# A decoder layer in one kernel: half steps in three segments, load buffers by stage, bank copies ordered ahead of splits

## The chip, the cores and the metric

The kernel runs on one core of a Trainium2 chip. The metric is the device time of one execution in microseconds (us). PE, DVE, ACT, POOL and SP are the names that the profile gives to TensorE, VectorE, ScalarE, GpSimd and SyncE; SP issues nearly all loads here.

## What is computed

Four steps act on x, 256 tokens of width 2048, in float32. The first and the last are SwiGLU half steps, and these two are what the change touches; an attention and gated-linear-attention mixer and a cross-attention lie between them.

```python
def swiglu(h, w_gate, w_up, w_down):
    return (jax.nn.silu(h @ w_gate) * (h @ w_up)) @ w_down

x = x + 0.5 * swiglu(rms_norm(x, ffn1_norm[l]), ffn1_w_gate[l], ffn1_w_up[l], ffn1_w_down[l])
x = x + hybrid_mixer(rms_norm(x, mix_norm[l]), pos, w_in[l], ...)
x = x + cross_attention(rms_norm(x, xattn_norm[l]), rms_norm(mem, mem_norm[l]), ...)
x = x + 0.5 * swiglu(rms_norm(x, ffn2_norm[l]), ffn2_w_gate[l], ffn2_w_up[l], ffn2_w_down[l])
```

The gate and up matrices are 2048 x 5632, the down matrix is 5632 x 2048.

## The kernel before

**Precision.** Each float32 operand is split in two parts of a narrower kind: `hi` is a cast (ACT) and `lo` the remainder (DVE). A product is three matmuls, hi by hi, hi by lo and lo by hi. So every 1 MB weight tile of 128 x 4 x 512 (a "raw" tile) is loaded, then split in two halves, each with one ACT cast into `wh` and one DVE subtraction into `wl` (`wgroup`, L127 and L128; `parts`, L174 and L175). There are four `wh` and four `wl` half buffers, so the splits run at most four halves ahead of PE.

**A half step** (`ffn`). The 5632 columns are eleven blocks f of 512. Block 0 is done plainly: a gate projection and an up projection (`proj`), eight raw tiles. The other ten go through `seven`: the upper half of the depth of gate and up is treated as a 2 x 2 block product in seven multiplications instead of eight. Write b11, b21 for the first two raw tiles of gate and b12, b22 for those of up. DVE adds b21, then b12, then b22 into b11 (`add`, L180), and POOL adds a tile from memory into b12 by a DMA (`add_hbm`, L184). In PE's order, the products P1 to P6 take b11+b21, b21, b11+b21+b12, b22, all four, and b12; four plain tiles follow, with a last product P7 on b12 before the fourth of them. A product is 12 matmuls of 128 x 128 by 512 columns and a plain tile 24, so a block has 180. Five of the products take differences of x blocks, which `differences` makes once per half step: POOL adds hi and lo of four x blocks (L212) and subtracts them in pairs (L217), ACT and DVE split the results `Fh`, `Fl` (L220, L221).

Four PSUM banks Y, Z, X, R collect the products. Between products Y is copied out by ACT (s21, L234; s22, L240; s12, L249), and DVE joins the banks (L245, L252, L253, L257). Then ACT takes silu of the gate (L366), DVE multiplies by the up part (L372), and `turn` transposes the result on PE (L343) and splits it as `hTh`, `hTl` (L261, L262), the left operand of the down projection.

**Segments.** `SEGS` does blocks 0 to 5, then their down projection in four column chunks, then blocks 6 to 10 and their down projection. At the end of a chunk DVE adds the two banks into x (L379). The turned blocks of a segment must stay in on-chip memory until its last chunk.

**What sets the order.** Each engine runs its own list in order, written by a scheduler from program order and priorities: weight loads and splits stand at `WPRI` = 200 ahead of program order, the first loads at 100000. `later(n, fn)` puts work n half-tiles back in PE's order; `turn` uses 1. A pool hands out buffers: `up` has 34 tiles of 2 KB per partition for everything of medium life, `wp` has `RB` = 5 raw tiles, from which b11, b12 and b22 come as well as the tiles that only pass through. A load waits on SP's list until its buffer is free, and the loads behind it wait too. At the start, ten warm-up matmuls (L413) run on a constant tile while the first loads are under way; x itself is loaded in four chunks at L434 for the norm factor r, which the first silu needs.

Of the kernel before, what the change touches and what calls it, by code (L numbers as in the profile page):

```python
# [27 lines left out]
WPRI = 200  # L28
WARM = 10
# [12 lines left out]
UB = 34  # L42
SB = 8
RB = 5
SEGS = (range(0, 6), range(6, NF))
# [3 lines left out]
def layer_kernel(ctx: ExitStack, tc: tile.TileContext, A: dict, out: bass.AP):  # L49
# [5 lines left out]
    up = ctx.enter_context(tc.tile_pool(name="up", bufs=UB))  # L55
# [4 lines left out]

    def U(shape, dt, name):
        return up.tile(shape, dt, tag="u", name=name)
# [30 lines left out]
    with tc.high_priority(100000):  # L93
        SY.dma_start(gain, A["gains"])
        for g in range(3):
            raw = wp.tile([P, 4, 512], F32, tag="raw", name="raw", bufs=RB)
# [64 lines left out]
    def load(W, c, g):  # L161
        with tc.high_priority(WPRI):
            raw = wp.tile([P, 4, 512], F32, tag="raw", name="raw", bufs=RB)
            SY.dma_start(raw, W[c, g])
        return raw
# [19 lines left out]

    def mms(bank, form, half, start, stop):
# [18 lines left out]
    def differences():  # L205

        x = {}
        for c in range(2):
            for t in range(TT):
                x[t, c] = U([P, 4, P], F32, "xf")  # L210
                hi, lo = (p[:, :, t * P:(t + 1) * P].bitcast(F32) for p in xT[c])
                G.tensor_tensor(x[t, c], hi, lo, op=ALU.add)  # L212
        r = {}
        for name, a, b in (("22-21", (1, 1), (1, 0)), ("12-21", (0, 1), (1, 0)), ("22-12", (1, 1), (0, 1)),
                           ("21-11", (1, 0), (0, 0)), ("11-12", (0, 0), (0, 1))):
            d = W2([P, 4, P], "d")
            G.tensor_tensor(d, x[a], x[b], op=ALU.subtract)  # L217
            hi = U([P, 4, P], F32R, "Fh")
            lo = U([P, 4, P], F32R, "Fl")
            SC.copy(hi, d)  # L220
            V.tensor_sub(lo, d, hi.bitcast(F32))  # L221
            r[name] = (hi, lo)
        return r

    def seven(W1, W2_, f, F, A12, A21, rest):


        Y, Z, X, R = [pa.tile([P, 512], F32, tag="acc", name="acc") for _ in range(4)]
        b11 = load(W1, f, 0)
        b21 = load(W1, f, 1)  # L230
# [3 lines left out]
        SC.copy(s21, Y)  # L234
        b12 = load(W2_, f, 0)
# [4 lines left out]
        SC.copy(s22, Y)  # L240
        b22 = load(W2_, f, 1)
# [3 lines left out]
        V.tensor_sub(s22, R, s22)  # L245
        product(Y, F["21-11"], b12, False)
        add_hbm(b12, W1[f, 0])
        s12 = W2([P, 512], "s12")
        SC.copy(s12, Y)  # L249
        for g in (2, 3):  # L250
            plain((R, X), (rest(0, g), rest(1, g)), load(W2_, f, g), (False, False), (1, 0))
        V.tensor_sub(s12, R, s12)  # L252
        V.tensor_add(s22, X, s22)  # L253
        plain((Y, Z), (rest(0, 2), rest(1, 2)), load(W1, f, 2), (False, False), (1, 0))
        product(Y, F["11-12"], b12, False)
        plain((Y, Z), (rest(0, 3), rest(1, 3)), load(W1, f, 3), (False, False), (0, 1))
        V.tensor_add(s21, Z, s21)  # L257
# [75 lines left out]
    def ffn(pre, r, after, fine=None, last=False):  # L333
        wg, wu, wd = (A[f"{pre}_w_{n}"] for n in ("gate", "up", "down"))
        hT = {}

# [12 lines left out]

        def lhs_h(k, t):  # L350
            return tuple(p[:, k % 4] for p in hT[k // 4, t])

        for seg in SEGS:
            for f in seg:
                if f == 0:
# [3 lines left out]
                    F = differences()  # L359
                else:  # L360
                    y, s21, s12, s22 = seven(wg, wu, f, F, x_block(0, 1), x_block(1, 0), x_block)
                    acc = [y, s21]
                sg = []
                for t in range(TT):
                    s = acc[t] if f and t else W2([P, 512], "sg")
                    SC.activation(s, acc[t], AF.Silu, scale=r[:, t:t + 1])  # L366
                    sg.append(s)
                acc = [s12, s22] if f else proj(wu, f, lhs_x, range(4))
                hs = []
                for t in range(TT):  # L370
                    h = acc[t] if f else W2([P, 512], "h")
                    V.scalar_tensor_tensor(h, acc[t], r[:, t:t + 1], sg[t], op0=ALU.mult, op1=ALU.mult)  # L372
                    hs.append(h)
                later(1, lambda f=f, hs=hs: turn(f, hs))
# [31 lines left out]
    mhalf = con.tile([P, P], F32, name="mhalf")  # L406
    V.memset(mhalf, -0.5)

# [598 lines left out]
```

## Time and profile before

| what | us |
|---|---|
| median of 3 runs (1962.8 to 1963.9) | 1963.34 |
| the profiled execution's own time | 1964.76 |
| its span, first to last instruction | 1962.7 |
| PE busy | 1933.6 |
| DVE busy | 1366.8 |
| ACT busy | 1064.6 |
| POOL busy | 110.6 |

The span is cut by the work as follows: the first block of the first half step and the way into `seven` fill 0 to 82 us; `seven` runs from 82 to 260, 422 to 600, 1302 to 1480 and 1641 to 1820; the down projections lie at 260 to 422, 600 to about 740, 1480 to 1641 and 1820 to the end; the mixer and the cross-attention lie between about 740 and 1240.

How to read it: matmuls overlap, so a matmul's own duration of 390 ns says little, and the distance from one start to the next says much. A busy share near 100% on PE hides matmuls that start late by a fraction of their length. In rows of the timeline, a bracket at the end gives the idle time of that engine before the instruction, and who ended it.

### The profile page before, as it was taken

The page shows a single profiled execution, that of the slowest core. Times are in us where ns is not written, and L with a number is a line of the kernel's source. Part 1 is how long each engine was busy: PE and PEld are TensorE (multiplying, and loading weights), DVE is VectorE, ACT ScalarE, POOL GpSimd, SP SyncE. Part 2 cuts the span into 40 slices and gives each one's busy share as a digit, 9 for nine tenths or more (in the row PEclk, how much of TensorE's full clock was granted, in tenths as well). Part 3 has the DMA queues.
Part 4 walks back from the last instruction along what each step waited for, and adds up shares of the span by engine and source line. Part 5 has one row for each costly group of instructions (what it writes and reads, how often), then busy time and mean ns, then how long its engine had stood idle before and what let it go on. Part 6 is the DMA issues. An engine that isn't in the chain of part 4 may idle for free.

```text
span 1962.7 us, 22466 instructions
## 1 busy us (share of the span) xinstructions
PE 1933.6 (99%) x8760; PEld 1582.1 (81%) x8760; DVE 1366.8 (70%) x1388; ACT 1064.6 (54%) x1305; POOL 110.6 (6%) x99
## 2 busy tenths in 40 slices
PE   8899999999999999999999999999999999999999
PEld 6688788888778888878888889778778888877887
DVE  6788874578887554646775665878886457888643
ACT  5556653355665445544576545656665335666532
POOL 4100000000000000001221000300000000000000
PEclk9899999999999999999999999999999999999999
DMA  8466565556667554535466553556657555666652
GB/s 343 153 211 236 195 238 194 194 207 216 220 209 241 204 182 154 178 129 209 172 215 214 188 184 143 178 190 232 210 199 256 193 193 194 229 202 212 237 214 84
DMA packets 60566, 395.24 MB, mean 201 GB/s; under 512 B 6795, under 2 KB 7947, under 8 KB 14252
## 3 DMA queue, kind: packets, MB, share of 16 engines
q1 hardware_dynamic: 56428, 370.74, 51.6%
q0 software_dynamic: 2880, 20.97, 5.8%
q10 hardware_dynamic: 1152, 2.10, 0.3%
q8 instruction: 68, 1.11, 0.2%
q14 instruction: 38, 0.31, 0.0%
HBM read 391.69 MB, written 2.10 MB: 201 GB/s over the span
## 4 chain that ended last, share of the span: by engine, by line
PE 68%; DVE 20%; DMA 6%; issue 5%; ACT 1%; SPq 0%; DVEq 0%; ACTq 0%
PE acc L138 17%; PE acc L136 17%; PE acc L137 17%; DVE wl L175 13%; DMA raw<-in_ffn_w_gate_dram 6%; PE acc L191 5%; PE acc L190 5%; PE acc L189 5%; DVE raw L180 3%; DVE s L372 1%; ACT wh L174 1%; DVE hTl L262 1%; DVE wl L128 1%; PE tp L343 0%; PE tp L302 0%
## 5 line engine op out<-in xcount | busy, mean ns | idle before, releaser
L128 DVE TENSOR_TENSOR wl<-raw,wh 128x1024 fp32r<-128x1024 f32 (+1 forms) x370 | 459.4, 1246 | 367.8 <-ACT wh L127 365.4
L127 ACT CAST wh<-raw 128x1024 fp32r<-128x1024 f32 (+1 forms) x370 | 386.5, 1048 | 441.0 <-PE acc L138 400.6
L174 ACT CAST wh<-raw 128x1024 fp32r<-128x1024 f32 x440 | 457.8, 1053 | 308.8 <-PE acc L191 274.6
L175 DVE TENSOR_TENSOR wl<-raw,wh 128x1024 fp32r<-128x1024 f32 x440 | 522.2, 1223 | 94.1 <-ACT wh L174 91.0
L189 PE MATMUL acc<-wh,xTh 128*128 128x512 f32 x800 | 314.4, 393 | 3.5 <-ACT sg L366 2.3
L190 PE MATMUL acc<-wl,xTh 128*128 128x512 f32 x800 | 314.2, 393 | 1.5 <-DVE wl L175 0.8
L191 PE MATMUL acc<-wh,xTl 128*128 128x512 f32 x800 | 313.6, 392 | 0.0
L136 PE MATMUL acc<-wh,hTh 128*128 128x512 f32 x704 | 274.6, 390 | 0.0
L138 PE MATMUL acc<-wh,hTl 128*128 128x512 f32 x704 | 274.0, 389 | 0.0
L137 PE MATMUL acc<-wl,hTh 128*128 128x512 f32 x704 | 274.0, 389 | 0.0
L136 PE MATMUL acc<-wh,xTh 128*128 128x512 f32 x544 | 215.0, 396 | 5.4 <-ACT wh L127 2.8
L137 PE MATMUL acc<-wl,xTh 128*128 128x512 f32 x544 | 212.5, 391 | 2.6 <-DVE wl L128 2.6
L138 PE MATMUL acc<-wh,xTl 128*128 128x512 f32 x544 | 212.0, 390 | 0.7 <-DVE xTl L286 0.7
L189 PEld LDWEIGHTS acc<-wh,xTh 128*128 128x128 f32 x800 | 150.4, 188 | 42.3 <-ACT wh L174 9.3
L190 PEld LDWEIGHTS acc<-wl,xTh 128*128 128x128 f32 x800 | 150.4, 188 | 40.0 <-DVE wl L175 9.3
L191 PEld LDWEIGHTS acc<-wh,xTl 128*128 128x128 f32 x800 | 150.5, 188 | 30.3
L180 DVE TENSOR_TENSOR raw<-raw 128x2048 f32<-128x2048 f32 x60 | 137.3, 2289 | 51.2 <-DMA raw<-in_ffn_w_gate_dram 50.5
L191 PE MATMUL acc<-wh,Fl 128*128 128x512 f32 x400 | 157.0, 393 | 4.1 <-DVE Fl L221 4.1
L190 PE MATMUL acc<-wl,Fh 128*128 128x512 f32 x400 | 158.8, 397 | 0.2 <-DVE wl L175 0.2
L189 PE MATMUL acc<-wh,Fh 128*128 128x512 f32 x400 | 157.6, 394 | 0.0
L137 PEld LDWEIGHTS acc<-wl,hTh 128*128 128x128 f32 x704 | 132.2, 188 | 27.4
L138 PEld LDWEIGHTS acc<-wh,hTl 128*128 128x128 f32 x704 | 132.1, 188 | 27.3
(281 smaller groups left out, 1946.5 us busy)
## 6 DMA issues: line engine op xcount, KB each, us to landing
raw<-in_ffn_w_up_dram SPq DMA_DIRECT2D x88, 1024.0 KB, 4.8
raw<-in_ffn_w_down_dram SPq DMA_DIRECT2D x88, 1024.0 KB, 4.8
raw<-in_ffn_w_gate_dram SPq DMA_DIRECT2D x85, 1024.0 KB, 4.9
raw<-in_w_in_dram SPq DMA_DIRECT2D x48, 1024.0 KB, 4.8
raw<-in_ffn_w_gate_dram POOLq DMA_DIRECT2D x20, 1024.0 KB, 9.3
raw<-in_w_out_dram SPq DMA_DIRECT2D x16, 1024.0 KB, 4.8
raw<-in_xattn_w_k_dram SPq DMA_DIRECT2D x4, 1024.0 KB, 5.7
raw<-in_xattn_w_q_dram SPq DMA_DIRECT2D x4, 1024.0 KB, 4.8
```

Source lines behind the costliest of these rows:

```text
L127: SC.copy(wh[:, d], src)
L128: V.tensor_sub(wl[:, d], src, wh[:, d].bitcast(F32))
L136: PE.matmul(acc[t], lh, wh, start=first and i == 0, stop=False)
L137: PE.matmul(acc[t], lh, wl, start=False, stop=False)
L138: PE.matmul(acc[t], ll, wh, start=False, stop=last and i == len(half) - 1)
L174: SC.copy(wh, src)
L175: V.tensor_sub(wl, src, wh.bitcast(F32))
L180: V.tensor_add(dst, dst, src)
L189: PE.matmul(bank, hi[:, k], wh, start=start and i == 0, stop=False, skip_group_check=True)
L190: PE.matmul(bank, hi[:, k], wl, start=False, stop=False, skip_group_check=True)
L191: PE.matmul(bank, lo[:, k], wh, start=False, stop=stop and i == len(half) - 1, skip_group_check=True)
L262: V.tensor_sub(lo, ps, hi.bitcast(F32))
```

## The change

- `SEGS` becomes three segments: blocks 0 to 3, 4 to 7 and 8 to 10, each with its down projection in four chunks.
- The pool for medium tiles is opened anew for each stage (`enter`): 26 tiles in the half steps with three more raw tiles beside them, 32 in the middle. `RB` goes from 5 to 4. b11, b12 and b22 come from the three (`raw_tile(long=True)`), everything else from the four.
- Loads of `seven` go from priority 200 to `LPRI` = 400.
- The bank copies and joins, the silu and the multiplication get priority `FPRI` = 300 (`urgent`), above the splits.
- The differences of x are made by DVE, additions and subtractions alike, three of them one half-tile after block 0's gate projection and two four half-tiles later; the last two are split into the x blocks (1,1) and (0,0) in place.
- `turn` is put back by 2 half-tiles instead of 1; the x chunks' load priorities fall by 12 per chunk instead of 34.
- The warm-up matmuls read a tile `idle` of their own, set by DVE.

```diff
-UB = 34
+UF = 26
+UM = 32
 SB = 8
-RB = 5
-SEGS = (range(0, 6), range(6, NF))
+RB = 4
+RX = 3
+DIFF = 1
+TURN = 2
+SEGS = (range(0, 4), range(4, 8), range(8, NF))
...
+    def raw_tile(long=False):
+
+        if long and "r" in stage:
+            return stage["r"].tile([P, 4, 512], F32, tag="rawx", name="raw")
+        return wp.tile([P, 4, 512], F32, tag="raw", name="raw", bufs=RB)
+
+    enter(u=UF, r=RX)
...
+    def urgent(op, *args, **kw):
+
+        with tc.high_priority(FPRI):
+            op(*args, **kw)
...
+    def difference(x, name, home=None):
+
+        a, b = PAIRS[name]
+        with tc.high_priority(WPRI):
             d = W2([P, 4, P], "d")
-            G.tensor_tensor(d, x[a], x[b], op=ALU.subtract)
-            hi = U([P, 4, P], F32R, "Fh")
-            lo = U([P, 4, P], F32R, "Fl")
+            V.tensor_sub(d, x[a], x[b])
+            hi, lo = home or (U([P, 4, P], F32R, "Fh"), U([P, 4, P], F32R, "Fl"))
             SC.copy(hi, d)
             V.tensor_sub(lo, d, hi.bitcast(F32))
...
-        b11 = load(W1, f, 0)
-        b21 = load(W1, f, 1)
+        b11 = load(ld(0, k1), True)
+        b21 = load(ld(0, k2))
         add(b11, b21)
         product(Y, A21, b11, True)
         s21 = W2([P, 512], "s21")
-        SC.copy(s21, Y)
-        b12 = load(W2_, f, 0)
+        urgent(SC.copy, s21, Y)
+        b12 = load(ld(1, k1), True)
...
-                    F = differences()
+                    later(DIFF, lambda: x_differences(("22-21", "12-21", "22-12")))
+                    later(DIFF + 4, lambda: x_differences(("21-11", "11-12")))
...
-                later(1, lambda f=f, hs=hs: turn(f, hs))
+                later(TURN, lambda f=f, hs=hs: turn(f, hs))
...
-        PE.matmul(wps, mhalf, mhalf, start=True, stop=True)
+        PE.matmul(wps, idle, idle, start=True, stop=True)
...
-            with tc.high_priority(XPRI - 34 * c):
+            with tc.high_priority(XPRI - 12 * c):
                 SY.dma_start(xs[c], A["x"][0, :, c * 512:(c + 1) * 512].rearrange("(t p) d -> p t d", p=P))
```

The scheduler's lists move at three places. The first is SP's list at the start, behind the loads of block 0's first three gate tiles, where both kernels are alike. Before (L117 loads a tile of block 0, L164 one of block 1, `xr` is the transposed x and `x_105` to `x_108` are the four x chunks):

```order
L117 DMA raw<-in_ffn_w_gate_dram 128x2048
L276 DMA xr<-in_xT_dram 128x512 x2
L434 DMA x_105<-in_x_dram 128x2x512
L117 DMA raw<-in_ffn_w_up_dram 128x2048 x2
L434 DMA x_106<-in_x_dram 128x2x512
L117 DMA raw<-in_ffn_w_up_dram 128x2048
L434 DMA x_107<-in_x_dram 128x2x512
L164 DMA raw<-in_ffn_w_gate_dram 128x2048 x2
L434 DMA x_108<-in_x_dram 128x2x512
L164 DMA raw<-in_ffn_w_up_dram 128x2048 x4
```

After (L189 loads for block 1, L142 for block 0, L304 is the transposed x, L480 the x chunks):

```order
L189 DMA raw<-in_ffn_w_gate_dram 128x2048
L189 DMA raw<-in_ffn_w_up_dram 128x2048 x2
L142 DMA raw<-in_ffn_w_gate_dram 128x2048
L304 DMA xr<-in_xT_dram 128x512 x2
L142 DMA raw<-in_ffn_w_up_dram 128x2048
L480 DMA x_108<-in_x_dram 128x2x512
L480 DMA x_109<-in_x_dram 128x2x512
L480 DMA x_110<-in_x_dram 128x2x512
L480 DMA x_111<-in_x_dram 128x2x512
```

Three tiles of block 1 (b11, b12, b22) now stand ahead of block 0's fourth gate tile and of the last quarter of the transposed x, and the x chunks stand closer behind them.

The second place is DVE's list at the passage from block 0 to block 1. Before, from the last split of block 0 to P3's first split (raw_523 is b11, raw_525 b21, raw_568 b12; `Fl_346` and `Fl_352` belong to P2 and P3):

```order
L128 TENSOR_TENSOR wl_500<-raw_481,wh_499 128x1024
L180 TENSOR_TENSOR raw_523<-raw_523,raw_525 128x2048
L322 TENSOR_REDUCE r1t_329<-ss1_308 128x2
...
L175 TENSOR_TENSOR wl_529<-raw_523,wh_528 128x1024
...
L175 TENSOR_TENSOR wl_581<-raw_525,wh_580 128x1024
L180 TENSOR_TENSOR raw_523<-raw_523,raw_568 128x2048
L221 TENSOR_TENSOR Fl_346<-d_343,Fh_345 128x512
L372 SCALAR_TENSOR_TENSOR h_515<-acc_377,r1_333,sg_373 128x512
L221 TENSOR_TENSOR Fl_352<-d_349,Fh_351 128x512
L175 TENSOR_TENSOR wl_592<-raw_523,wh_591 128x1024
```

After, over the same stretch (raw_524 is b11, raw_526 b21, raw_569 b12):

```order
L350 TENSOR_REDUCE r1t_334<-ss1_313 128x2
...
L243 TENSOR_TENSOR d_372<-xf_370,xf_366 128x512
...
L246 TENSOR_TENSOR Fl_375<-d_372,Fh_374 128x512
...
L246 TENSOR_TENSOR xTl0_140<-d_462,xTh0_139 128x4x128
L153 TENSOR_TENSOR wl_501<-raw_482,wh_500 128x1024
L205 TENSOR_TENSOR raw_524<-raw_524,raw_526 128x2048
L214 SCALAR_TENSOR_TENSOR h_516<-acc_344,r1_338,sg_340 128x512
L214 SCALAR_TENSOR_TENSOR h_518<-acc_345,r1_338,sg_342 128x512
L200 TENSOR_TENSOR wl_530<-raw_524,wh_529 128x1024
...
L205 TENSOR_TENSOR raw_524<-raw_524,raw_569 128x2048
L290 TENSOR_TENSOR hTl_550<-tp_551,hTh_549 128x512
...
L200 TENSOR_TENSOR wl_593<-raw_524,wh_592 128x1024
```

All five differences and their remainders now stand ahead of the first addition for block 1, and both multiplications of block 0 stand ahead of P1's first split.

The third place is DVE's list where one block of `seven` ends and the next begins, the third block to the fourth. Before (raw_1173 is b11 of the fourth block, s12_1003 and s22_936 are the third's results):

```order
L180 TENSOR_TENSOR raw_1173<-raw_1173,raw_1218 128x2048
L175 TENSOR_TENSOR wl_1221<-raw_1175,wh_1220 128x1024
L257 TENSOR_TENSOR s21_891<-acc_845,s21_891 128x512
L372 SCALAR_TENSOR_TENSOR s12_1003<-s12_1003,r1_333,sg_1164 128x512
L175 TENSOR_TENSOR wl_1231<-raw_1175,wh_1230 128x1024
L175 TENSOR_TENSOR wl_1242<-raw_1173,wh_1241 128x1024
L372 SCALAR_TENSOR_TENSOR s22_936<-s22_936,r1_333,s21_891 128x512
L175 TENSOR_TENSOR wl_1252<-raw_1173,wh_1251 128x1024
L262 TENSOR_TENSOR hTl_1189<-tp_1190,hTh_1188 128x512
```

After, the same stretch:

```order
L205 TENSOR_TENSOR raw_1174<-raw_1174,raw_1219 128x2048
L200 TENSOR_TENSOR wl_1222<-raw_1176,wh_1221 128x1024
L214 SCALAR_TENSOR_TENSOR s12_1004<-s12_1004,r1_338,sg_1165 128x512
L214 TENSOR_TENSOR s21_892<-acc_846,s21_892 128x512
L200 TENSOR_TENSOR wl_1232<-raw_1176,wh_1231 128x1024
L200 TENSOR_TENSOR wl_1243<-raw_1174,wh_1242 128x1024
L214 SCALAR_TENSOR_TENSOR s22_937<-s22_937,r1_338,s21_892 128x512
L200 TENSOR_TENSOR wl_1253<-raw_1174,wh_1252 128x1024
L290 TENSOR_TENSOR hTl_1200<-tp_1201,hTh_1199 128x512
```

Only the first multiplication and the join of s21 have changed places. In PE's list the transposes of s12 move from behind the eighth matmul of P1 to behind its twelfth, and those of s22 keep their place in P2; the ten warm-up matmuls move from the head of the list to behind the 31st matmul.

96 lines of the change are left out of this document (59 added, 37 removed).

## The prediction

> **What bounds the kernel now.** I read the page first, then the list of waits on PE, the table by stage, and the timelines of the two stages that lose time.
>
> ```profile
> PE 1933.6 (99%) x8760; PEld 1582.1 (81%) x8760; DVE 1366.8 (70%) x1388; ACT 1064.6 (54%) x1305; POOL 110.6 (6%) x99
> ```
>
> PE is busy for 1933.6 of 1962.7 us, so it is the bound, and what a change of order can win is the 29 us of idle PE and matmuls that start late inside its busy time. The table by stage shows where these are.
>
> ```profile
> 0.00:58.00 58.00, 49.91 (x211) 38.76 (x212) 41.36 (x35) 32.85 (x53) 27.83 (x25) 1.00 0.81 309
> 58.00:82.00 24.00, 17.33 (x59) 12.83 (x58) 18.87 (x19) 13.30 (x18) 0.00 (x0) 0.79 0.24 88
> 82.00:260.00 178.00, 176.94 (x784) 142.65 (x783) 153.98 (x138) 111.67 (x124) 4.49 (x5) 1.00 0.65 220
> 260.00:422.00 162.00, 162.00 (x720) 134.06 (x719) 90.42 (x81) 68.58 (x69) 0.00 (x0) 1.00 0.56 200
> 600.00:1230.00 630.00, 630.00 (x3020) 525.26 (x3020) 378.28 (x502) 340.47 (x505) 50.52 (x45) 1.00 0.53 187
> ```
>
> The columns are PE, PE's loads, DVE, ACT and POOL busy, then PE's granted clock, the DMA share and GB/s. From 600 to 1230 and in a down projection (260 to 422) PE has no gap: nothing is to be won there, and DVE is busy for only 90 of 162 us. In `seven` (82 to 260) DVE is busy for 154 of 178 us, and from 58 to 82 PE idles 6.7 us at a mean clock of 0.79. PE's waits name the causes.
>
> ```profile
> PE tp L343 <- DVE s L372: 5.4, 8, 0.9
> PE acc L191 <- DVE Fl L221: 4.1, 1, 4.1
> PE acc L189 <- ACT sg L366: 2.3, 1, 2.3
> PE acc L189 <- ACT wh L174: 0.6, 2, 0.3
> ```
>
> **The passage from block 0 to block 1.** In PE's timeline a matmul's start to the next start is what counts.
>
> ```profile
> 14.28 0.73 PE L136 MATMUL acc<-wh,xTh 128*128 128x512 f32 x2 [1.31 <-ACT wh L127]
> 60.78 0.50 PE L189 MATMUL acc<-wh,xTh 128*128 128x512 f32 x1 [2.30 <-ACT sg L366]
> 62.65 0.63 PE L190 MATMUL acc<-wl,xTh 128*128 128x512 f32 x1
> 63.08 0.63 PE L191 MATMUL acc<-wh,xTl 128*128 128x512 f32 x1
> 73.86 0.79 PE L191 MATMUL acc<-wh,Fl 128*128 128x512 f32 x1 [4.14 <-DVE Fl L221]
> 76.29 0.63 PE L191 MATMUL acc<-wh,Fl 128*128 128x512 f32 x1
> 331.04 0.39 PE L138 MATMUL acc<-wh,hTl 128*128 128x512 f32 x1
> 331.27 0.39 PE L136 MATMUL acc<-wh,hTh 128*128 128x512 f32 x1
> ```
>
> At 331 matmuls start 0.23 us apart, at 62.65 and 63.08 0.43 apart. About eight slow ones follow the 2.30 us gap and about ten the 4.14 us gap: 1.6 and 2.0 us on top of the gaps. The 1.31 us gap at 14.28 had no such price: the granted clock from 10 to 20 us is 1.00 (row further below).
>
> The 4.14 us gap is P3 waiting for a remainder of a difference, which came late from POOL and then stood behind an addition on DVE:
>
> ```profile
> 53.21 3.53 POOL L217 TENSOR_TENSOR d<-xf 128x512 f32<-128x512 f32 x2
> 70.92 2.29 DVE L180 TENSOR_TENSOR raw<-raw 128x2048 f32<-128x2048 f32 x1
> 73.12 0.68 DVE L221 TENSOR_TENSOR Fl<-d,Fh 128x512 fp32r<-128x512 f32 x1
> 88.69 0.57 ACT L249 COPY s<-acc 128x512 f32<-128x512 f32 x1
> ```
>
> P6 ends when the copy of s12 begins, at 88.7; block 0 ended at about 58.4 (60.78 less the gap). So the first six products took 30.3 us, where 72 matmuls and eight transposes need 72 x 0.227 + 0.8 = 17.1.
>
> After the change all differences are done on DVE before P1. Count from U, the end of block 0 on PE. DVE's list has two multiplications, which wait for U, then P1's first split: 1.5 + 1.2, so P1 runs freely from U+2.7, a gap like today's 2.30, with 1.6 us of slow clock (kept). Ahead of P3 DVE has, behind that split, three more splits, the addition of b12, two hTl and P3's own: 4 x 1.22 + 2.29 + 2 x 0.68 = 8.5, so U+11.2. PE needs 24 x 0.227 + 0.8 + 1.6 = 7.9 and comes at U+10.6: 0.6 us of waiting instead of 4.14. P5 needs three more splits, the addition of b22 and its own: 4 x 1.22 + 2.29 = 7.2, U+18.4, where PE comes at U+16.6. P5 and P6 take 5.4, so P6 ends at U+23.8: 6.5 us less than today. The wait of 1.8 us before P5 lies between the 1.31 us that left the clock alone and the 2.30 us that slowed it: 0 to 1.6 us more, of which I take half. That leaves **5.7 us**. [...]
>
> What moves U is the front of SP's list: 3 MB of block 1 go ahead of block 0's fourth gate tile and the last x quarter.
>
> ```profile
> 10.00:20.00 10.00, 7.67 (x32) 5.31 (x31) 7.84 (x9) 6.20 (x9) 6.52 (x5) 1.00 1.02 407
> 20.00:30.00 10.00, 7.48 (x31) 5.18 (x29) 10.00 (x6) 3.69 (x5) 10.00 (x6) 1.00 1.04 427
> 27.30 4.00 POOL L284 TENSOR_TENSOR xr<-xr,gain 128x512 f32<-128x512 f32 x2
> 30.02 0.50 PE L136 MATMUL acc<-wh,xTh 128*128 128x512 f32 x1 [0.98 <-ACT xTh L285]
> ```
>
> At 0.42 MB/us the 3.1 MB cost 7.5 us. Today the fourth group starts at 30.0 because POOL, busy with x additions, scales the last x quarter only from 27.3; those additions leave POOL. By bytes in order, 9.5 MB must land before that quarter is there; some 6 MB have landed at 20, so it is there at 28, POOL and ACT add 1.3 and 0.6: again 30. U stays, within -1 and +5 (the bound if it lands 5 us later).
>
> The additions and subtractions, 4 + 5, cost DVE 0.68 each (L221's price) and lie beside block 0, where POOL's took 1.8 us each (the row at 53.21). Today DVE itself slows beside them:
>
> ```profile
> L128 DVE TENSOR_TENSOR wl<-raw,wh 128x1024 fp32r<-128x1024 f32 x14 | 22.4, 1629 | 6.9 <-ACT wh L127 6.9
> L175 DVE TENSOR_TENSOR wl<-raw,wh 128x1024 fp32r<-128x1024 f32 x85 | 100.3, 1218 | 9.4 <-ACT wh L174 8.8
> ```
>
> A split means 1629 ns up to 62 us and 1218 ns from 100 to 260.
>
> ```profile
> 1.06 4.02 PE L413 MATMUL wps<-mhalf 128*128 128x128 f32 x20 [1.06 <-DVE mhalf L407]
> ```
>
> The warm-up takes 4.0 us before any data is there; behind the 31st matmul it takes between 2 (at twice the clock) and 4, and the fourth group's data, not before 28, covers it: PE's work up to there is 72 matmuls, 16 us, begun at 6.3. If that cover goes, +2 to +4. In the second half step the differences lie beside block 0 as well: 0, within -1 and +2.
>
> **One block to the next in `seven`.** The transposes of s12 mark the blocks: first and last of four in the first run, then of four in the last run.
>
> ```profile
> 113.86 0.66 PE L343 MATMUL tp<-ident,s 128*128 128x128 f32 x4
> 242.61 0.63 PE L343 MATMUL tp<-ident,s 128*128 128x128 f32 x4 [0.65 <-DVE s L372]
> 1677.46 0.63 PE L343 MATMUL tp<-ident,s 128*128 128x128 f32 x4
> 1807.78 0.63 PE L343 MATMUL tp<-ident,s 128*128 128x128 f32 x4 [0.85 <-DVE s L372]
> ```
>
> A passage means from one such row to the next: a block takes 42.9 and 43.4 us, mean 43.2; 180 x 0.227 + 0.8 is 41.6. So 1.6 us are lost per block, over 16 such passages. DVE's timeline before the row at 242.61 shows why:
>
> ```profile
> 227.44 2.29 DVE L180 TENSOR_TENSOR raw<-raw 128x2048 f32<-128x2048 f32 x1 [3.30 <-DMA raw<-in_ffn_w_gate_dram]
> 237.77 2.29 DVE L180 TENSOR_TENSOR raw<-raw 128x2048 f32<-128x2048 f32 x1
> 241.12 0.68 DVE L257 TENSOR_TENSOR s<-acc,s 128x512 f32<-128x512 f32 x1
> 241.72 0.74 DVE L372 SCALAR_TENSOR_TENSOR s<-s,r,sg 128x512 f32<-128x512 f32 x1
> ...
> 251.55 0.68 DVE L262 TENSOR_TENSOR hTl<-tp,hTh 128x512 fp32r<-128x512 f32 x1
> ```
>
> ```profile
> DVE raw L180 <- DMA raw<-in_ffn_w_gate_dram: 50.5, 17, 4.1
> ```
>
> DVE waits 3.30 us for the next block's first tiles and then never idles until P5; over the kernel 17 such waits make 50.5 us. With four passing buffers and three long ones those tiles are there in time, so this wait goes. It is not all gain: the splits behind it are soon held by ACT, which follows PE's buffers, so the addition at 237.77 comes only about 0.8 us sooner. The multiplication at 241.72 comes 0.6 earlier again (it goes before the join), and the transposes come four matmuls later: their wait of 0.65 to 0.85 goes. What is late next are P4's and P5's splits, still behind two additions and two hTl; PE, coming earlier, waits there about as long as the lead doesn't cover. I take 0.5 us per passage, between 0 (all given back) and 1.3 (all but what transposes cost by themselves). Fourteen passages give 7, the two that vanish with the third segment 0.5 each: **8 us**, between 0 and 19.
>
> The bank copies cost nothing: ACT takes each as the product before it ends, and the cast behind it waits for a buffer of that same product. The third segment adds 16 accumulations of 0.74 us on DVE, hidden in down projections where it is idle by half, and two more starts of `seven`, at 0.3 us of PE each (the two waits for L174's cast in PE's list above are such starts): +0.6, between 0 and 2.
>
> ```profile
> raw<-in_w_in_dram SPq DMA_DIRECT2D x48, 1024.0 KB, 4.8
> ```
>
> In the rest `RB` is 4 and the medium tiles are 32: a tile lands 4.8 us after its issue, PE works 24 x 0.227 = 5.4 us on one, and four are under way. So 0; if a load that waits for a medium tile holds SP's list for longer than the 16 us of work in the other three, that excess, which nothing in the trace shows.
>
> **Sum.** -5.7 - 8 + 0.6 = -13.1. The profiled execution's 1964.76, of which the span is 1962.7, would become 1951.7; the median stands 1.4 below it, so about 1950 for the runs.
>
> **Rivals.**
> 1. All waits in `seven` go: 14 x 1.3 + 1 = 19 and the passage into block 1 its 6.5, so 1938. For it speaks that DVE is busy for only 87% of the stage, against it that it is full from 227 to 256. Chance 0.1.
> 2. DVE, full, gives back all that the transposes win; only the passage into block 1 is won: 1958. Of the first four rows of transposes only the last waited, and the mean of 42.9 is still 1.3 above 41.6, which speaks for it. Chance 0.18.
> 3. The early 3 MB push U back by 5 us, which leaves 0.7 of that passage, and `seven` gives 2: about 1961, no change. For it: loads ran at 407 to 427 GB/s only when nothing waited for buffers. Chance 0.12.
> 4. Slower: the joins that now stand ahead of splits. The subtraction of R (s22) comes before the next plain tile's four splits; it waits for P5's end. Then P6 runs 2.7 us, and subtraction and split take 0.7 + 1.2: 0.8 us to spare. If another 2 us (a remainder, a late cast) stand between, each block loses 1.2 us, over half of the 20 or all of them +12 to +24; less the 5.7, 1970 to 1982, say 1976. It decides from 0.8 us on. Against it: the split's cast is ready by then. Chance 0.1.
>
> **Numbers.** My forecast 1950 has 0.5. Runs of this kernel tell 0.2%, 3.9 us, from no change. Faster (under 1959.4): 0.5, 0.1 and most of 0.18, less a tail: 0.74. Same: rival 3 and the edge of 2: 0.16. Slower (over 1967.3): 0.1. The range from 1938 to 1962 takes in rivals 1 to 3 and leaves out the fourth and tails.
>
> **What would show it.** Right: no PE wait of 4 us for Fl, P6 of block 1 about 24 us behind block 0's end; the additions in `seven` without a wait for DMA; no transposes waiting for L214; passages at 42.7. The fourth gate group starts near 30. Wrong: a wait of PE on xTh beyond 33, passages still at 43.2, or new waits of PE on `wl` of the first plain tile.

## The result, and the profile after

The changed kernel takes **1977.97 us** (median of 4 runs, 1976.90 to 1978.33); the kernel before, in the same session, 1963.62. The ratio is 1.0070, with a 95% interval of 1.0053 to 1.0088: slower by 0.7%, where 1950 and faster was forecast, and outside the range of 1938 to 1962. The profiled execution took 1978.33, with a span of 1976.2, 13.5 more than before's 1962.7.

The first line of the page, busy times of the engines:

```profile
PE 1951.9 (99%) x8760; PEld 1582.7 (80%) x8760; DVE 1377.3 (70%) x1423; ACT 1062.0 (54%) x1305; POOL 78.9 (4%) x81
```

PE has as many instructions as before, 8760, but is busy for 18.3 us longer. It waits less, as the change meant it to, and works longer on the same work. From the list of PE's waits:

```profile
PE acc L161 <- ACT wh L152: 6.1, 1, 6.1
PE acc L220 <- DVE wl L200: 4.9, 7, 0.8
PE acc L161 <- ACT xTh L313: 2.3, 1, 2.3
PE tp L868 <- ACT un L860: 1.6, 2, 1.3
PE tp L372 <- DVE h L214: 0.2, 1, 0.2
```

The 6.1 us are the first load of the kernel (before, the warm-up lay there). The 4.1 us for `Fl` are gone, and of the transposes' 5.4 us 0.2 are left. New are the waits for a remainder `wl`, seven instead of two and up to 0.8 us each (three in block 1, four in the first block behind a down projection), and two for `un`, a tile of the cross-attention.

**Where the longer work is.** Two rows of the table by stage for the kernel before, then for the changed one. The columns are those of the prediction: the stretch, its length, PE, PE's loads, DVE, ACT and POOL busy, PE's clock, DMA share and GB/s. The first row of each is one down projection (576 wide matmuls before, 384 after, a wide one having 512 columns, and eight transposes near its head; the row's ends cut into one or two more), the second `w_out`, the mixer's output projection, whose left operand is called mT.

```profile
283.30:414.90 131.60, 131.60 (x585) 108.89 (x584) 69.05 (x61) 52.23 (x51) 0.00 (x0) 1.00 0.52 188
1070.00:1161.00 91.00, 91.00 (x419) 75.70 (x418) 56.47 (x65) 47.97 (x69) 3.56 (x3) 1.00 0.56 198
```

```profile
457.00:547.50 90.50, 90.50 (x394) 72.67 (x392) 49.70 (x45) 35.22 (x35) 0.00 (x0) 1.00 0.52 180
1075.70:1172.60 96.90, 94.38 (x417) 75.17 (x417) 53.54 (x62) 47.58 (x71) 3.62 (x3) 1.00 0.50 177
```

PE has no gap in either down projection, the clock is 1.00 in both, and the DMA share is the same. From the first matmul to the first one behind it the two take 131.64 and 90.48 us. Less 0.98 and 0.79 for the transposes, a matmul takes 130.66 / 576 = 0.2268 us before and 89.69 / 384 = 0.2336 after. The groups of the two pages show the same thing by operand (count | busy, mean ns of one | idle before); first before, then after:

```profile
L189 PE MATMUL acc<-wh,xTh 128*128 128x512 f32 x800 | 314.4, 393 | 3.5 <-ACT sg L366 2.3
L136 PE MATMUL acc<-wh,hTh 128*128 128x512 f32 x704 | 274.6, 390 | 0.0
```

```profile
L219 PE MATMUL acc<-wh,xTh 128*128 128x512 f32 x960 | 375.9, 392 | 0.7
L161 PE MATMUL acc<-wh,hTh 128*128 128x512 f32 x704 | 278.3, 395 | 0.0
L163 PE MATMUL acc<-wh,hTl 128*128 128x512 f32 x704 | 277.5, 394 | 0.0
L162 PE MATMUL acc<-wl,hTh 128*128 128x512 f32 x704 | 277.5, 394 | 0.0
```

The matmuls whose stationary operand is xT kept their time; those on hT, which lies in the pool `u`, went from 390 to 395 ns. So it is no wait, no clock and no traffic that all matmuls would share.

**The balance.** Between the first matmuls of the stages in PE's timelines (192 wide matmuls are block 0, 180 each other block):

| | before | after | difference |
|---|---|---|---|
| start to the first matmul | 6.3 | 6.1 | -0.2 |
| blocks 0 and 1, first half step | 54.5 + 51.2 | 56.9 + 47.7 | -1.1 |
| blocks 0 and 1, second half step | 46.6 + 43.6 | 45.5 + 42.4 | -2.3 |
| blocks 2 to 10, both | 771.3 | 767.3 | -4.0 |
| down projections, both | 486.0 | 500.9 | +14.9 |
| mixer | 499.0 | 505.3 | +6.3 |
| sum | | | +13.6 |

The blocks, from which the prediction expected its gain, gained 7.4 us. The down projections and the mixer, which it put at +0.6 and at nothing, lost 21.2.

### The profile page after: what moved, and what is told of

It reads as the page before. It is cut to its first block, busy times and chain, and to the rows that moved or that the text cites. A ratio compares the mean times of both kernels' runs of the same rounds, so it can differ in the third digit from the quotient of the medians.

```text
span 1976.2 us, 22472 instructions
## 1 busy us (share of the span) xinstructions
PE 1951.9 (99%) x8760; PEld 1582.7 (80%) x8760; DVE 1377.3 (70%) x1423; ACT 1062.0 (54%) x1305; POOL 78.9 (4%) x81
## 3 DMA queue, kind: packets, MB, share of 16 engines
q10 hardware_dynamic: 1152, 2.10, 0.3%
## 4 chain that ended last, share of the span: by engine, by line
PE 81%; DVE 12%; issue 3%; DMA 2%; ACT 2%; POOL 0%; SPq 0%; ACTq 0%; POOLq 0%
PE acc L161 17%; PE acc L163 17%; PE acc L162 17%; PE acc L220 9%; PE acc L221 9%; PE acc L219 9%; DVE wl L200 7%; DVE raw L205 2%; DMA raw<-in_ffn_w_gate_dram 2%; DVE s L214 1%; ACT wh L199 1%; DVE hTl L290 1%; PE tp L330 0%; DVE wl L153 0%; PE tp L372 0%
## 5 line engine op out<-in xcount | busy, mean ns | idle before, releaser
L153 DVE TENSOR_TENSOR wl<-raw,wh 128x1024 fp32r<-128x1024 f32 (+1 forms) x370 | 452.5, 1226 | 377.0 <-ACT wh L152 375.0
L220 PE MATMUL acc<-wl,xTh 128*128 128x512 f32 x960 | 375.8, 391 | 5.0 <-DVE wl L200 4.1
L219 PE MATMUL acc<-wh,xTh 128*128 128x512 f32 x960 | 375.9, 392 | 0.7
L221 PE MATMUL acc<-wh,xTl 128*128 128x512 f32 x960 | 373.7, 389 | 0.0
L161 PE MATMUL acc<-wh,xTh 128*128 128x512 f32 x544 | 217.0, 399 | 8.4 <-ACT wh L152 6.1
L220 PEld LDWEIGHTS acc<-wl,xTh 128*128 128x128 f32 x960 | 180.2, 188 | 50.0 <-DVE wl L200 13.0
L219 PEld LDWEIGHTS acc<-wh,xTh 128*128 128x128 f32 x960 | 180.2, 188 | 45.8 <-ACT wh L199 8.9
L163 PE MATMUL acc<-wh,xTl 128*128 128x512 f32 x544 | 214.3, 394 | 0.9 <-DVE xTl L314 0.9
L162 PE MATMUL acc<-wl,xTh 128*128 128x512 f32 x544 | 214.6, 394 | 0.3 <-DVE wl L153 0.3
L221 PEld LDWEIGHTS acc<-wh,xTl 128*128 128x128 f32 x960 | 180.2, 188 | 37.0
L205 DVE TENSOR_TENSOR raw<-raw 128x2048 f32<-128x2048 f32 x60 | 137.3, 2289 | 55.3 <-DMA raw<-in_ffn_w_gate_dram 54.6
L161 PEld LDWEIGHTS acc<-wh,hTh 128*128 128x128 f32 x704 | 131.7, 187 | 32.0
L161 PEld LDWEIGHTS acc<-wh,xTh 128*128 128x128 f32 x544 | 103.5, 190 | 30.9 <-ACT wh L152 6.1
L163 PEld LDWEIGHTS acc<-wh,xTl 128*128 128x128 f32 x544 | 103.4, 190 | 23.0 <-DVE xTl L314 1.3
```

What stands on the lines that cost most here:

```text
L153: V.tensor_sub(wl[:, d], src, wh[:, d].bitcast(F32))
L161: PE.matmul(acc[t], lh, wh, start=first and i == 0, stop=False)
L162: PE.matmul(acc[t], lh, wl, start=False, stop=False)
L163: PE.matmul(acc[t], ll, wh, start=False, stop=last and i == len(half) - 1)
L205: V.tensor_add(dst, dst, src)
L219: PE.matmul(bank, hi[:, k], wh, start=start and i == 0, stop=False, skip_group_check=True)
```

## The experiments

**Place of the tiles.** In these rows no matmul waits and the clock is full, so the new order of the lists doesn't explain a longer distance from one to the next. What the diff also did was to take the medium tiles out of their pool behind `wp` and to open `u` behind the pools of small tiles, and to make the constant `mhalf` smaller, so all tiles have other addresses. The allocator's list says: hT, wh and wl began at 256 modulo 2048 bytes before; afterwards hT at 1888, wh and wl at 1568. xT went from 1536 to 1056. Four kernels move tiles alone, and their instructions stay the same. In the diffs `pool(n)` is short for `ctx.enter_context(tc.tile_pool(name=n, bufs=1))`; nothing uses the tile in it.

`b_u96`, the kernel before with hT, mT and Fh moved by 96 bytes (and the pools behind them by 128):

```diff
-    up = ctx.enter_context(tc.tile_pool(name="up", bufs=UB))
+    pad = pool("pad"); pad.tile([P, 24], F32)      # 96 bytes
+    up = ctx.enter_context(tc.tile_pool(name="up", bufs=UB))
+    pad2 = pool("pad2"); pad2.tile([P, 8], F32)    # 32 bytes
```

> The kernel before with 96 empty bytes ahead of the pool up and 32 behind it: only its tiles (hT, mT, Fh) move, from a multiple of 128 bytes to 96 above one, where the changed kernel has them. Theory: hT's 2112 matmuls and those on mT go from 0.227 to 0.234, and the time rises by about 20 us to 1984 (1978 to 1988). Rival of traffic and segments: 1963.6, no change.

`a_all32`, the changed kernel with all tiles behind the constant moved by 32; `a_u32` and `a_u64`, with only the stage pools moved:

```diff
-    mhalf = con.tile([P, 8], F32, name="mhalf")
+    mhalf = con.tile([P, 16], F32, name="mhalf")        # a_all32
     st = ctx.enter_context(tc.tile_pool(name="st", bufs=10))
+    pad = pool("pad"); pad.tile([P, 8], F32)            # a_u32 (16: a_u64)
```

> The changed kernel with 32 bytes more in the first pool (the constant -0.5 is 128x16 instead of 128x8), so that every tile behind it lies 32 bytes further and all tiles that PE reads again begin at a multiple of 64 bytes, as in the kernel before; no instruction moves. Theory (the place of PE's operands in SBUF): matmuls on hT go back from 0.234 to 0.227 us from start to start, mT and Fh too, and the time falls by about 20 us to 1958 (1954 to 1962). Rival (the third segment and the traffic beside the down projections slow PE): 1978, and 0.234 on hT stays. Second rival (what counts is the distance between the stationary and the moving tile, which this edit leaves as it is): 1978 too.

> The changed kernel with an empty pool of 32 bytes ahead of the stage pools, so that only the tiles of u and r (hT, mT, Fh, long raw buffers) lie 32 bytes further, at multiples of 64 bytes; wh, wl and xT stay 32 bytes off. Theory: hT's matmuls 0.227, the time about 1958 to 1960. If it is the moving tiles wh and wl that must be aligned: 1978 as without the edit. Rival of traffic: 1978.

> The changed kernel with an empty pool of 64 bytes ahead of the stage pools: hT, mT, Fh lie 64 bytes further, still 32 bytes off a multiple of 64, but now 32 above a multiple of 128 like the tiles of xT, whose matmuls did not slow; before they lay 96 above one. Theory in the form 'off a multiple of 64': no change, 1978 and 0.234. Theory in the form 'the second half of 128 bytes': hT's matmuls 0.227 and about 1958. Rival of traffic: 1978.

Measured: `b_u96` 1985.12 (ratio to before 1.0112, 1.0095 to 1.0129), `a_all32` 1977.49, `a_u32` 1980.16, `a_u64` 1976.48. The first down projection of `b_u96`, beside the 131.60 of before:

```profile
283.10:419.00 135.90, 135.90 (x586) 109.29 (x585) 69.30 (x61) 52.15 (x51) 0.00 (x0) 1.00 0.50 182
```

96 bytes alone cost the old kernel 22 us, with its two segments, its loads and its order: the rival of segments and traffic falls. But a multiple of 64 or 128 bytes does not help the changed kernel, so the theory as I had put it falls too. What fits these four, before and after is the distance between the stationary tile and the moving tiles wh and wl, modulo 256 bytes: 0 before; 64 after and in `a_all32` (both 0.2336 us for a matmul on hT); 96 in `a_u32` and `b_u96` (0.2345 and 0.2343); 128 in `a_u64` (0.2326). xT lay at a whole multiple of 256 from wh in both kernels. Three kernels test that: `a_u192` sets the distance to 0, `b_all96` moves everything and keeps it, `b_w96` moves wh, wl and the raw tiles by 96 and what lies behind them by a whole 256.

```diff
     st = ctx.enter_context(tc.tile_pool(name="st", bufs=10))
+    pad = pool("pad"); pad.tile([P, 48], F32)           # a_u192, on the changed kernel
-    mhalf = con.tile([P, P], F32, name="mhalf")
+    mhalf = con.tile([P, P], F32, name="mhalf"); con.tile([P, 24], F32)   # b_all96, on before
+    pad = pool("pad"); pad.tile([P, 24], F32)           # b_w96, on before: ahead of wp,
     wp = ctx.enter_context(tc.tile_pool(name="wp", bufs=3))
+    pad2 = pool("pad2"); pad2.tile([P, 40], F32)        # and 160 bytes behind it
```

> The changed kernel with an empty pool of 192 bytes ahead of the stage pools: hT, mT and Fh then lie at a whole multiple of 256 bytes from wh and wl (31 above one plus 1: both 32 above a multiple of 256). The runs so far give a matmul on hT, start to start, by that distance modulo 256: 0 0.2268 us, 64 0.2336 (twice, with the tiles at 352 and at 384), 96 0.2345 and 0.2344, 128 0.2326. Theory (the distance between stationary and moving tile counts): hT 0.2268, and the time falls by 2112 x 0.0068 = 14, by about 6 on mT and by 1 to 3 on Fh and the rest: 1955 (1952 to 1959). Rival (a multiple of 64 or 128 bytes of the stationary tile itself counts, with some further condition): 32 above a multiple of 64, so 1978.

> The kernel before with 96 empty bytes in the first pool: xT, wh, wl, hT, mT all lie 96 bytes further, hT where it was slow (352 modulo 2048), but all distances stay. Theory of the distance: 1963, no change, hT at 0.227. Rival (the stationary tile's own address): hT at 0.234 as when it was moved alone, 1985 or, with xT slowed too, more.

> The kernel before with 96 empty bytes ahead of the weights' pool and 160 behind it: wh, wl and the raw buffers move by 96 bytes, xT stays and hT moves by 256, so every stationary tile keeps its place modulo 256, and its distance to the moving one is 160. Theory of the distance: all of about 7,900 wide matmuls slow by 0.006 to 0.0077 us, those on xT too: +47 to +61, 2010 to 2024. Rival (the stationary tile's own address): 1963.

Measured: `a_u192` 1961.33 (0.9997, 0.9988 to 1.0005), `b_all96` 1962.63 (1.0003, 0.9994 to 1.0012), `b_w96` 2000.56 (1.0199, 1.0185 to 1.0213). The second down projection of `a_u192`, beside 90.50 of the changed kernel; then, of `b_w96`, the first down projection and the first part of the mixer, whose stationary operand is xT (before: the row shown above, and 302.9 us for that part, from 741.5 to 1044.4):

```profile
454.60:542.50 87.90, 87.90 (x393) 72.89 (x392) 49.45 (x45) 35.35 (x35) 0.00 (x0) 1.00 0.52 186
```

```profile
285.10:420.50 135.40, 135.40 (x585) 108.94 (x584) 69.20 (x61) 51.90 (x51) 0.00 (x0) 1.00 0.50 182
752.10:1062.10 310.00, 310.00 (x1425) 248.88 (x1424) 190.90 (x288) 172.61 (x260) 43.42 (x35) 1.00 0.47 171
```

All three come out for the distance. hT at 352 modulo 2048 is slow alone (`b_u96`) and free when wh moves with it (`b_all96`); xT at its old place becomes slow when wh moves away from it (7.1 us over 1152 wide matmuls, 0.006 each). `b_w96` lost 39 us and not 47 to 61, because in `seven` part of the slower work fills what were waits: a block takes 43.4 us there, only 0.4 more than before's mean. `a_u192` gained 16.6 and not 23; what is left is in `w_out` and at the start.

It is not an access of DVE or ACT that slows PE either. In the changed kernel's second down projection the matmuls start 0.2335 us apart while DVE is idle and ACT works, and 0.2335 while ACT is idle and DVE works; in `a_u192` they are 0.2268 and 0.2267 apart.

**The medium tiles and the first loads.** In `a_u192` `w_out` still took 95.0 us against 90.7 before. In the changed kernel x's transposes (L330) stand at the end of `w_out`, behind those of `un`, which wait (rows of PE's timeline after); before they stood between its chunks (rows of before).

```profile
1159.05 0.33 PE L868 MATMUL tp<-ident,un 128*128 128x128 f32 x1 [0.34 <-ACT un L860]
1162.36 0.59 PE L868 MATMUL tp<-ident,un 128*128 128x128 f32 x3 [1.29 <-ACT un L860]
1163.30 1.80 PE L330 MATMUL tp<-ident,x 128*128 128x128 f32 x15
```

```profile
1095.56 1.03 PE L302 MATMUL tp<-ident,x 128*128 128x128 f32 x8
1118.23 1.03 PE L302 MATMUL tp<-ident,x 128*128 128x128 f32 x8
```

`un` needs the norm of mem, whose loads go into medium tiles, and SP's list after has two of these eight loads behind twelve more tiles of `w_out`. `a_um34` gives the middle 34 of these again. `a_u192_g4` leaves that and takes the fourth gate tile and the last x quarter ahead of block 1's 3 MB; `a_g4_um34` has both.

```diff
-UM = 32
+UM = 34                       # a_um34, a_g4_um34
-        for g in range(3):
+        for g in range(4):    # a_u192_g4, a_g4_um34
```

> As a_u192 (the 192-byte pool), and the stage pool u of the middle has 34 tiles again instead of 32. With 34 the list puts the loads of mem (L839), the statistics of mem and the transposes of x back where the kernel before has them, between the chunks of w_out; with 32 they stand at the end of w_out. Theory: the waits there (three of 0.38 us on x, two of 0.56 and 1.29 us on un, and the slow matmuls behind them) go, w_out takes 90.7 us instead of 95.0, and the time is 4 us under a_u192, about 1957. Rival (the waits come from something else, as the third segment's use of the banks): 1961 as a_u192.

> As a_u192, and the loads of the fourth gate tile and the last x quarter of block 0 go ahead of the 3 MB of block 1, by letting the first loop of loads run over four groups instead of three. Theory (the early 3 MB held the fourth group to 31.2 us, and the 2.28 us gap before it halved PE's clock for 6 us): the gap and the slow matmuls go, block 0 ends 5 to 7 us earlier than 62.7, and the time is 5 to 7 us under that of a_u192, about 1949. Rival (block 1's tiles then come late for its first product): a wait of 2 to 7 us of PE at block 1 takes it back, equal to a_u192.

> As a_um34, and the loads of the fourth gate tile and the last x quarter ahead of block 1's 3 MB (as in a_u192_g4). If the three causes (place of the tiles, the order of the first loads, the number of medium tiles) are independent: 1961.3 - 4.1 - 2.7 = 1954.5. If they share a cover: 1957 to 1958.

Measured: `a_um34` 1956.21 (0.9972, 0.9962 to 0.9981), `a_u192_g4` 1958.60 (0.9982, 0.9973 to 0.9990), `a_g4_um34` 1951.85 (0.9951, 0.9939 to 0.9964). In `a_um34` the transposes are back between the chunks, `w_out` takes 90.7 us and the mixer 498.1 instead of 502.8:

```profile
1091.58 1.04 PE L330 MATMUL tp<-ident,x 128*128 128x128 f32 x8
1114.25 1.04 PE L330 MATMUL tp<-ident,x 128*128 128x128 f32 x8
```

In `a_u192_g4` the gap of 2.28 us at 31.16 is gone, with the half clock behind it (granted 0.50 from 32.32 to 39.15 in the changed kernel), but the gain is 2.7 us against the 5 to 7 expected: PE now waits three times for 0.4 to 0.7 us in the first groups and has the warm-up (2.3 us) in its way. With `a_um34` as the base the same edit is worth 4.4. The first block differs by some 2 us between executions of kernels that start alike (55.2 us in `a_um34`, 57.1 in `a_u192`; the clock there is halved for 3.41 and for 6.83 us), so these two figures can't be told apart.

`a_warm` puts the warm-up first again, as it was before:

```diff
-    idle = U([P, P], F32, "idle")
-    V.memset(idle, -0.5)
-        PE.matmul(wps, idle, idle, start=True, stop=True)
+        PE.matmul(wps, mhalf, mhalf, start=True, stop=True)   # mhalf is 128x128 again
```

> As a_g4_um34, and the ten warm-up matmuls read the constant of 512 bytes as in the kernel before, so that they stand first in PE's list instead of behind its 31st matmul. In a_u192_g4 the first matmuls ran at 0.43 us and more from 6.15 to 11.4, and the warm-up took 2.3 us of PE from 23.5 to 25.8 while its data was there. Theory (both now cost PE time, since the fourth group no longer waits for its data): 2.5 to 5 us less, 1950 to 1952. Rival (the fourth group waits for its data again, which hides both): no change, 1954.5, with a wait of 2 us or more for xTh.

Measured: 1951.19 (0.9949, 0.9936 to 0.9961), no more than 0.7 below `a_g4_um34`. Neither expectation names what happened: the first groups wait for their data, and behind two gaps, of 1.28 and 1.02 us, matmuls start 0.42 us apart.

```profile
13.71 0.73 PE L161 MATMUL acc<-wh,xTh 128*128 128x512 f32 x2 [1.28 <-ACT wh L152]
15.46 0.51 PE L162 MATMUL acc<-wl,xTh 128*128 128x512 f32 x1 [1.02 <-DVE wl L153]
16.44 0.63 PE L162 MATMUL acc<-wl,xTh 128*128 128x512 f32 x1
16.86 0.63 PE L163 MATMUL acc<-wh,xTl 128*128 128x512 f32 x1
17.29 0.63 PE L162 MATMUL acc<-wl,xTh 128*128 128x512 f32 x1
```

**The wait on which the prediction's second step rested.** In the changed kernel DVE still waits for b21 as long as before (50.5 us, 17 times):

```profile
DVE raw L205 <- DMA raw<-in_ffn_w_gate_dram: 54.6, 14, 4.7
```

`a_rb5` takes this wait away, with a fifth passing buffer:

```diff
-UF = 26
-RB = 4
+UF = 22
+RB = 5
```

> As a_um34, but five passing raw buffers instead of four, and 22 tiles in u in the FFN stages instead of 26, which make the room. The additions of b11 and b21 then get their tile one buffer earlier; in the changed kernel DVE waited 54.6 us for it, 14 times. The prediction's step (this wait goes, and with it half a microsecond per block): DVE's wait under 15 us and the time 4 to 8 us under a_um34, 1949 to 1953. Rival (DVE's wait costs PE nothing, since DVE makes it up before P4): DVE's wait goes and the time stays within 2 us of a_um34. Second rival (22 tiles are too few for u, and a turn waits for a free one): slower.

Measured: 1954.86 (0.9965, 0.9953 to 0.9978), 1.4 below `a_um34`, with overlapping intervals. The list of DVE's waits has no more DMA row for L205; its first two rows are:

```profile
DVE wl L153 <- ACT wh L152: 345.2, 270, 4.4
DVE wl L200 <- ACT wh L199: 136.3, 126, 1.7
```

and a block that doesn't open a segment takes 42.6 to 42.7 us, with the wait and without it. The first rival is right: 53 us of waiting on DVE cost PE nothing.

**The curve, and whether the causes add.**

```diff
+    pad.tile([P, 56], F32)     # a_u224: distance 32
+    pad.tile([P, 32], F32)     # a_u128: distance 192
-UM = 32
+UM = 34                        # a_um_only: the changed kernel without a pad
```

> The changed kernel with an empty pool of 224 bytes ahead of the stage pools: hT, mT and Fh begin at a multiple of 64 bytes and lie 32 bytes above a whole multiple of 256 from wh and wl. If the price rises evenly from 0 at distance 0 to 0.0068 us at 64: half of it, hT at 0.230 and 1969. If only the whole multiple is free: hT at 0.233 to 0.235 and about 1977. If 32 bytes are still free: 1961 as with 192.

> The changed kernel with an empty pool of 128 bytes: the distance is 192 modulo 256, as far below a whole multiple as the changed kernel's 64 is above one. If the price is even on both sides: hT at 0.2336 and 1978. If it falls from 128 (0.2326) and 160 (0.2335 in b_w96) to 0 at 256: hT between 0.228 and 0.231, 1966 to 1971.

> The changed kernel with 34 medium tiles instead of 32 and nothing else: w_out's transposes stand between its chunks as before, hT and mT stay at 64 from a multiple of 256. If the causes add: 1978 less 4 to 5, 1973 to 1974, w_out about 93.2 instead of 96.9. If the waits were only a sequel of the slow matmuls: 1978.

Measured: `a_u224` 1977.55, `a_u128` 1966.76, `a_um_only` 1973.74. The second down projections of `a_u224` and of `a_u128`:

```profile
456.90:547.40 90.50, 90.50 (x394) 73.00 (x393) 49.70 (x45) 35.27 (x35) 0.00 (x0) 1.00 0.50 180
```

```profile
455.40:544.20 88.80, 88.80 (x393) 72.95 (x392) 49.59 (x45) 35.29 (x35) 0.00 (x0) 1.00 0.50 183
```

With 0.8 us for the transposes taken off and the rest divided by 384, for the changed kernel moved by its pad:

| distance modulo 256 bytes | 0 | 32 | 64 | 96 | 128 | 192 |
|---|---|---|---|---|---|---|
| us from matmul to matmul | 0.2269 | 0.2335 | 0.2336 | 0.2345 | 0.2326 | 0.2292 |
| kernel, us | 1961.3 | 1977.6 | 1978.0 | 1980.2 | 1976.5 | 1966.8 |

The price is not even on both sides: 32 bytes above a whole multiple cost nearly all of it, 64 below one a third. The times of the last line come from several sessions, in which the kernel before itself had medians of 1961.8 to 1963.6. The medium tiles take 4.1 us off the mixer without the pad (`a_um_only`, 505.3 to 501.1) and 4.7 with it (502.8 to 498.1): the two causes add, to within 0.6 us.

## Why the prediction was wrong

**The step that failed** is the one on the rest of the kernel: "From 600 to 1230 and in a down projection (260 to 422) PE has no gap: nothing is to be won there", and for the middle with fewer buffers, "So 0". I took a stage in which PE never waits for one with a fixed price, and looked only for waits that could appear. The down projections lost 14.9 us and the mixer 6.3. Of these, `a_u192` gives back 13.9 in the down projections (500.9 to 487.0) and 2.5 in the mixer by addresses alone; `a_um34` another 4.7 in the mixer, 0.9 more than was lost there. For these 4.7 the prediction had named a condition close to the cause, a load that waits for a medium tile, and given it no price. No row of before shows a matmul at another distance, so the size was not to be had from it; that the diff moves every tile was to be seen.

**Passage into block 1.** Forecast: P6 ends 23.8 us behind the end of block 0. Measured: block 0 ends at 62.8, where its transposes and P1 begin, and ACT's copy of s12 begins at 86.45: 23.7, against 30.4 before. The rows of PE's timeline, and the copy:

```profile
62.77 0.49 PE L372 MATMUL tp<-ident,h 128*128 128x128 f32 x3
63.01 0.48 PE L219 MATMUL acc<-wh,xTh 128*128 128x512 f32 x1
71.65 0.50 PE L219 MATMUL acc<-wh,Fh 128*128 128x512 f32 x1 [1.15 <-ACT wh L199]
72.91 0.50 PE L220 MATMUL acc<-wl,Fh 128*128 128x512 f32 x1 [0.76 <-DVE wl L200]
80.91 0.50 PE L220 MATMUL acc<-wl,xTh 128*128 128x512 f32 x1 [0.61 <-DVE wl L200]
86.45 0.59 ACT L214 COPY s<-acc 128x512 f32<-128x512 f32 x1 [0.30 <-PE acc L221]
```

The sum is right, its parts are not: P1 starts 0.25 us behind block 0 and not 2.7, P3 waits 1.9 and not 0.6 and is followed by half clock (0.50 from 73.28 to 76.69), P5 waits 0.6 and not 1.8. And "U stays" was wrong: block 0 ended 4.4 us later, near the bound of 5 that I gave.

```profile
31.16 0.50 PE L161 MATMUL acc<-wh,xTh 128*128 128x512 f32 x1 [2.28 <-ACT xTh L313]
33.04 0.80 PE L163 MATMUL acc<-wh,xTl 128*128 128x512 f32 x1 [0.95 <-DVE xTl L314]
33.63 0.63 PE L161 MATMUL acc<-wh,xTh 128*128 128x512 f32 x1
38.75 0.58 PE L161 MATMUL acc<-wh,xTh 128*128 128x512 f32 x1
```

The fourth group starts 1.1 us later than before's 30.02, which I had as "again 30"; what I had not costed is the half clock behind the gaps there: granted 0.50 from 32.32 to 39.15, 0.43 us from matmul to matmul between 33.6 and 38.8, 2.4 us for the twelve. Of the forecast 5.7 us, blocks 0 and 1 kept 1.1. Rival 3 had U late by the early 3 MB, at a price of 5 us and with 0.12; its price fits, but the late data are 1.1 us of it. How much half clock followed was not the same in every kernel (last section): in `a_rb5`, with a gap of 1.66 us there, none did (0.23 us from matmul to matmul from 32.71 on), and block 0 took 53.4 us. In the second half step the same two blocks gained 2.3, where I had 0.

**One block to the next.** Forecast: passages of 42.7 us. Measured: 42.6 to 42.7 in every block that doesn't follow a down projection, against 42.6 to 43.6 and 43.0 on average before. But the two blocks behind a down projection took 41.4 before, and the four now take 42.5, so nine blocks, twice, gained 4.0 and not 8. The cause that I gave for the gain (DVE's wait for the load goes) is wrong twice over: the wait stayed, and `a_rb5` shows that it cost nothing. That the gain in the later blocks is the transposes' wait, 5.4 us before and 0.2 after, fits its size (14 x 0.4) but was not tested. The third segment costs 0.5 us in each half step's down projections once the addresses are right (244.8 against 244.3, and 242.2 against 241.7), and the dearer starts above: in each of the four, PE waits at P5 for its first split (0.77 us of idle time at 299.22, 560.21, 1527.66 and 1788.64); before, the only idle time in the first blocks behind a down projection was 0.28 us each.

**The rivals.** The fourth named 1976 and slower, by joins ahead of splits. The time fits, the mechanism does not: the blocks in `seven` got shorter. With the three causes undone (`a_g4_um34`) the change has a span of 1949.6, 13.1 under before's, which is the sum that I forecast. Its parts are others: blocks 0 and 1 -6.3 (forecast -5.7) and, in the second half step, -2.3 (0), blocks 2 to 10 -4.4 (-8), down projections +1.0 (+0.6), mixer -0.9 (0). So the sum came out by errors that cancel.

## What to carry to other kernels

When a diff opens pools in another order or changes the size of a constant, compare the tiles' addresses before and after, and put what PE reads as stationary operand at a whole multiple of 256 bytes from what it reads as moving one. (Measured here for float32 tiles with 512 bytes of stationary operand per partition and matmul: 0.2269 us from matmul to matmul there, up to 0.2345 at the other distances.) In a stage in which an engine is busy throughout the price per instruction can change, as it did in the down projections here (0.2268 us before, 0.2336 after): look at start-to-start times there too, not at waits alone. A long wait of an engine that is not the bound (53 us of DVE here) is no gain until an experiment without it says so.

## What the runs showed of the hardware

- In these runs a wide matmul started 0.2269 us behind the one before it with its two operands at a multiple of 256 bytes from one another, and up to 0.2345 us at the other distances, at a granted clock of 1.00 in both cases. The loads of the weights on hT kept their time, a mean of 188 ns before and 187 after. 96 bytes of distance cost 22 us in `b_u96`. What causes it no run here shows.
- The granted clock changed only on a grid: within one trace all its changes lie at whole multiples of 3.41 us from one another (in the changed kernel's the stretches between them are 6.83, 34.13 and 3.41 us long in the first 77 us), and the grid lies differently against the start of each execution, by 0.87 us before, 1.61 after and 2.49 in `a_g4_um34`. Half clock went with PE's idle share of such a window. In the traces of all 17 kernels, 30 windows at full clock have PE idle for half of their length or more, and 29 of them are followed by half clock (the other is one of 55% in `b_w96`); of the windows with less, up to 47%, none is. In the first 100 us and behind PE's first matmul they begin, in the kernel before, at 58.89 and 69.13, with PE idle for 55 and 85%, and in the changed kernel at 28.91 and 69.87, with 73 and 56%. Two neighbouring windows each of the changed kernel, of `a_g4_um34` and of before show it:

```profile
69.87:73.28 3.41, 1.50 (x6) 0.71 (x5) 3.41 (x5) 2.73 (x3) 0.00 (x0) 1.00 0.67 279
73.28:76.69 3.41, 3.41 (x10) 2.65 (x9) 3.41 (x4) 1.17 (x2) 0.00 (x0) 0.50 0.00 0
```

```profile
63.93:67.34 3.41, 1.82 (x7) 0.94 (x5) 3.41 (x4) 1.95 (x3) 0.00 (x0) 1.00 0.83 308
67.35:70.75 3.40, 3.00 (x13) 2.51 (x14) 3.40 (x4) 2.12 (x4) 0.00 (x0) 1.00 0.00 0
```

```profile
11.11:14.52 3.41, 2.10 (x9) 1.36 (x9) 1.57 (x3) 1.56 (x2) 2.25 (x2) 1.00 1.03 408
14.52:17.93 3.41, 2.38 (x10) 1.65 (x10) 3.41 (x3) 2.58 (x4) 2.20 (x3) 1.00 1.05 429
```

The two gaps ahead of P3 are nearly the same in the first two kernels, 1.15 and 0.76 us and 1.23 and 0.76. In the changed kernel both fall into one window, PE is busy for 1.50 of its 3.41 us, and the next runs at 0.50; in `a_g4_um34` the second gap is shared between two windows, PE is busy for 1.82 us, and the clock stays. In the same way 1.31 and 1.02 us in the kernel before fall into two windows and cost nothing, and 1.28 and 1.02 in `a_warm` almost wholly into one. So in these traces no length of gap by itself tells it. That the same kernel can pay in one execution and not in the next is my inference from the grid; with one trace of each kernel it was not shown.

- Without the warm-up ahead, the changed kernel's first twelve matmuls start 0.43 us apart and more, from 6.1 to 11.4; behind the warm-up those of before start 0.23 apart from 7.4 on, where data did not hold them up.
